# A decoder layer on one core: row dots moved from retrieval into the gate units, a gelu behind one more tile, and fewer row fetches beside two-layer tiles

## The chip, the cores and the metric

The kernel runs on one core of a Trainium2 chip. The core has five engines with instruction streams of their own: TensorE (PE; its weight loads are listed apart as PEld), VectorE (DVE), ScalarE (ACT), GpSimd (POOL) and SyncE (SP, which here only issues transfers). Each works its stream in order and waits for the others by semaphores. The metric is the device time of one execution in microseconds (us).

## The reference, cut to what matters

The layer is a token mixer (pooling, sparse attention, cross-attention) followed by a PEER channel mixer. The change lies in the latter. For 512 tokens and 8 heads it finds the 16 best of 16,384 single-neuron experts, and adds up their outputs:

```python
def block(xb):                       # tokens xb, n of them
    q = (xb @ w_q).reshape(n, PEER_HEADS, 2, PEER_HALF)
    s = jnp.einsum('nhpc,hpkc->nhpk', q, sub_keys)
    s_top, i_top = lax.top_k(s, PEER_TOPK)
    ...                              # the 16 best sums of two halves, their ids
    gate = jax.nn.softmax(best_s, axis=-1)
    u_e = u[ids]
    act = jax.nn.gelu(jnp.einsum('nd,nhkd->nhk', xb, u_e), approximate=False)
    wgt = gate * act
    return jnp.einsum('nhk,nhkd->nd', wgt, v[ids])
x = x + peer_ffn(rms_norm(x, g_ffn), ...)
```

## The kernel before, in words

The kernel computes the PEER mixer in two ways at once. The first 128 tokens (block 0) and, for the first layer only, 48 more tokens are **gathered**: the 128 rows of `u` that a token chose are fetched by indirect transfers, and DVE forms the dot products. For all other tokens (384, less the 48 in the first layer) the mixer is computed **densely**: each of 128 tiles of 128 experts is multiplied with all tokens on PE, and a gate that is zero for every expert not chosen is multiplied in.

A dense tile has a first layer, `hidden` (L172: 24 matmuls of 336 columns, then a gelu on ACT, L1226), and a second layer, 18 matmuls of 512 columns (L1656). Every float32 weight tile is split for PE into a high half `wh` (ACT, L144) and a low half `wl` (DVE or POOL, L145). The first layer of 80 tiles is done ahead, by the generator `lead()`; its results `hg` are stored in `hd`. These are **led tiles**; `step(1)` runs one. They fill PE while DVE does other things. In the last part, `experts()`, the 48 tiles not led come first (**two-layer tiles**), then the 80 led ones, of which only the second layer is left (**one-layer tiles**).

The order of the program around the change is written out by hand:

- *Retrieval.* For each of four blocks of tokens, `retrieve(b)` turns the top-k positions into expert ids on DVE in four pieces (L1342 to L1380); between them `step(1)` runs led tiles. The ids of the 48 tokens go out and come back turned, and POOL gathers their rows `ux` (L1420), 4 buffers ahead.
- *Dots.* `dot_x()` is one DVE instruction of 128x1024 (L1428) that multiplies one such row tile with the tokens and sums it into one column of `actx`; then POOL gathers the row tile four further on. There are 48 dots.
- *Gate units.* The 384 tokens are cut into 12 units of 32. `one_hots` builds one-hot tables on DVE (`oa` L1480, `ob` L1484 and twice L1487), and calls one function after each of the first three. `gates` multiplies them on PE (64 matmuls, L1497) for the unit before, ACT evicts the result (L1500), and a transfer that ACT issues stores it (L1508). Units 0 to 9 are without the 48 tokens (`plain` is 10); unit 9 is the last one before the gelu of `actx` is needed. Units 0 to 6 run five led tiles each, units 7 and 8 four.
- *Gelu of the dots.* `act_x()` is a gelu of `actx` on ACT (L1432). `regroup_x`, `gate_x` and `turn_x` then fold it into the gates of the 48 tokens.
- *Experts.* `weave` runs two generators beside each other, each with a weight: it always continues the one that is least far, by the sum of what it yielded over its weight. `experts()` yields 1.35 twice for a two-layer tile and 1.0 for a one-layer tile. `gathered(0)` yields 1 for each of its 262 row steps: it issues a row gather `ug` on POOL (L1520) and, six steps later, uses the row on DVE, first 128 rows of `u` (dot, L1534), then 128 rows of `v` (added into `x1g`, L1540).

For one tile, `experts()` multiplies the gates with `hg` on DVE (`gh`, L1635), splits the product (`wgh` on ACT L144, `wgl` on DVE L145), and splits the V tile; PE's second layer waits for these. `G` (`gj`, `go`) holds gates that come back from `gd`. The gathers of `gathered` begin behind a POOL copy `seen` that waits for the third V tile.

Of the kernel before, what the change touches and what calls it, by code (L numbers as in the profile page):

```python
# [36 lines left out]
def weave(*streams):  # L37

    live = [[0.0, w, iter(gen)] for gen, w in streams]
    while live:  # L40
        item = min(live, key=lambda x: x[0])
        try:
            c = next(item[2])
            item[0] += (c if c else 1.0) / item[1]
        except StopIteration:
            live.remove(item)
# [7 lines left out]
def seq(*gens):  # L54
    for x in gens:
        yield from x
# [65 lines left out]
def layer(ctx: ExitStack, tc: tile.TileContext, A: dict, out: bass.AP, dbg=None):  # L122
# [88 lines left out]
    GB = 1  # L211
# [3 lines left out]
    LEAD = 80  # L215
# [389 lines left out]
    for c in cross_order:  # L605
        n = int(c[1]) if c[1:].isdigit() else None
# [802 lines left out]
    todo_x, HX, PICK = list(range(X)), {}, []  # L1409
# [13 lines left out]
    def dot_x():  # L1423
        if not todo_x:
            return
        k = todo_x.pop(0)
        row = XR.pop(k)
        v.scalar_tensor_tensor(row, row, 1.0, HX[k >= 32], op0=OP.mult, op1=OP.mult, accum_out=actx[:, k:k + 1])  # L1428
        gather_x(k + XB)

    def act_x():
        s.activation(actx, actx, AF.Gelu)  # L1432
# [37 lines left out]
    def one_hots(u, *others):  # L1470
        others = iter(others)
        tk = slice(u * UT, u * UT + UT)
        full = [128, UT // 2, 128, 2]

        def pairs(x):
            return x.rearrange("p (a w) -> p a w", w=2)[:, :, None].to_broadcast(full)

        every = io128[:, None].to_broadcast(full)
        oa = gp.tile(full, F16, name="oa", bufs=2)
        v.tensor_tensor(oa, pairs(iT[:, tk]), every, op=OP.is_equal)  # L1480
        next(others)()
        ob = gp.tile([128, 2, 4096], F16, name="ob", bufs=2).rearrange(
            "p r (a j w) -> p r a j w", a=UT // 2, j=128)
        v.tensor_tensor(ob[:, 1], pairs(jT[:, tk]), every, op=OP.is_equal)  # L1484
        for r in range(2):
            next(others)()
            v.tensor_tensor(ob[:, r], ob[:, 1], pairs(gT[:, r, tk]), op=OP.mult)  # L1487
        return oa, ob

    def gates(u, oa, ob, then=None):  # L1490
        stg = sgp.tile([128, 64, UT, 2], F32, name="stg", bufs=2)
        for q_ in range(UT // 4):
            pg = psum(("S", "o", "tr")[(u * (UT // 4) + q_) % 3], [128, 4, 128])
            for n in range(4):
                t_ = q_ * 4 + n
                for r in range(2):
                    pe.matmul(pg[:, n], oa[:, t_ // 2, :, t_ % 2], ob[:, r, t_ // 2, :, t_ % 2],  # L1497
                              start=n == 0 and r == 0,
                              stop=n == 3 and r == 1, skip_group_check=True)
            s.activation(stg[:, :, q_ * 4:q_ * 4 + 4].rearrange("p j t c -> p t j c"),  # L1500
                         pg.rearrange("p t (j c) -> p t j c", c=2), AF.Copy, scale=1.0 / 32768.0)
            if then and q_ == 5:
                then()
        if u == 0:
            g.tensor_copy(own, stg[:, LEAD // 2:LEAD // 2 + 4])

        def store():
            s.dma_start((gd[:, :, u - 1] if u else gz).rearrange("j i x -> i j x"),  # L1508
                        stg.rearrange("p (j q) t c -> p j (q t c)", q=4))
        if u == 0:  # L1510
            return store
        store()
# [96 lines left out]
    def experts():  # L1609
        acc_o.extend(psum(("S", "S", "tr", "tr", "o", "o")[i], [128, 512]) for i in range(2 * ND))  # L1610
        for n in range(-1, 128):
            m = n + 1
            if m < 128:
                j = order[m]
                if j >= LEAD:
                    U[m] = feed.take(("u", j))
                vfetch(m + 3)
                hfetch(m + 4)
                if m == 8:
                    bcast_row(gl, A["g_final"])  # L1620
                if m == 100:
                    ex_[0].tile([128, 8], F32, name="pad")
                    for b in range(GB, NB):
                        X1[b] = (X1B if b == GB
                                 else uf.tile([128, D], F32, tag="wr", name="wr", bufs=2))
                        nc.sync.dma_start(X1[b], x1d[b - GB])
                if m % 8 == 4 and m + 4 < 128:
                    gload(m // 8 + 1)
                if j >= LEAD:
                    vpart(m)  # L1630
                    yield 1.35
                    H[m] = hidden(U.pop(m))
                gh = GH.pop() if GH else ex_[0].tile([128, NT], F32, name="gh", bufs=2)
                idle.append(H[m])
                v.tensor_tensor(gh.rearrange("p (g t) -> p g t", t=UT), G[m // 8][:, :, m % 8 // 2, :, m % 2],  # L1635
                                H.pop(m).rearrange("p (g t) -> p g t", t=UT), op=OP.mult)
                if j < LEAD:
                    yield 1.0
                wh = WGH.pop() if WGH else ex_[0].tile([128, NT], F32R, name="wgh", bufs=3)
                wl = ex_[0].tile([128, NT], F32R, name="wgl", bufs=3)  # L1640
                split(wh, wl, gh)
                if j < LEAD:
                    vpart(m)
                V[m] = (wh, wl, V[m])
                if j >= LEAD:
                    yield 1.35
            if n < 0 or n == 126:
                continue

            ends = n == 127  # L1650
            for b in range(ND):
                for k, hs in [(k, (half,)) for half in range(2) for k in (126, 127)] if ends else [(n, range(2))]:
                    wh, wl, vw = V[k]
                    for i, (a, c) in enumerate(((wh, vw[0]), (wl, vw[0]), (wh, vw[1]))):
                        for half in hs:
                            pe.matmul(acc_o[2 * b + half], a[:, b * 128:(b + 1) * 128], c[:, half],  # L1656
                                      start=k == 0 and i == 0, stop=k == 127 and i == 2)
                    if ends and k == 127:
                        closing(GB + b, hs[0])
                        if b and hs[0] == 0:  # L1660
                            finish(GB + b - 1)
                        if b and hs[0]:
                            for half in range(2):
                                output(GB + b - 1, half)
            V.pop(n)
# [12 lines left out]
    def step(n):  # L1678
        for _ in range(n):
            next(ld, None)  # L1680
# [14 lines left out]
    for n, b in enumerate(found):  # L1695
        for i, _ in enumerate(retrieve(b)):
            if n == 0 and i == 1:
                late.append(exp)
            if n or i:
                step(1)  # L1700
            if n == 3 or n == 2 and i:
                dot_x()
            if i in ((2, 3) if n == 0 else (1, 3)):
                piece()
        if n == 0:
            gate_softmax()
            lead_q[0] = nc.sync
        elif found[n - 1] >= GB:
            turn_sel(found[n - 1])
    pend = None  # L1710
# [7 lines left out]
    units = [*range(2, NT // UT), 1, 0]  # L1718
    plain = len(units) - 2
# [4 lines left out]
    def go_dot():  # L1724
        step(1)
        dot_x()

    for n, u in enumerate(units):
        def before():
            if n == plain:  # L1730
                regroup_x()
                gate_x()
            gates(units[n - 1], *pend)
            step(1)
            if n == plain:
                turn_x()

        if n >= plain:
            pend = one_hots(u, go, before, go)
            continue  # L1740
        oh_ = one_hots(u, go, go_dot if n < 7 else dot_x, go)
        if n == 0:
            turn_sel(NB - 1)
            step(1)
        dot_x()
        if n == plain - 1:
            while todo_x:
                dot_x()
        if pend is not None:
            gates(units[n - 1], *pend, act_x if n == plain - 1 else None)  # L1750
        step(1)
        if n < plain - 1:
            dot_x()
            step(1)
            dot_x()
        pend = oh_
    lead_q[0] = s
    step(1)
# [2 lines left out]
    gath = seq(*[gathered(b) for b in range(GB)])  # L1761
# [21 lines left out]
    vfetch(2)  # L1783
    g.tensor_copy(G[0][:, 0], own)
    g.tensor_copy(seen[:, 0:1], VR[2][:, 0:1])
    weave((experts(), 2.7 * (128 - LEAD) + 1.0 * LEAD), (gath, 268 * GB))
    finish(NB - 1)
    for half in range(2):
        output(NB - 1, half)
# [87 lines left out]
```

## Time and profile before

| | us |
|---|---|
| median of 3 runs | 1822.11 (1821.51 to 1822.67) |
| the profiled execution, in all | 1820.59 |
| its span, first to last instruction | 1818.8 |
| PE busy | 1780.1 (98%) |
| DVE busy | 1377.1 (76%) |
| ACT busy | 827.1 (45%) |
| POOL busy | 821.9 (45%) |

The mean granted clock of TensorE is 0.995. By the profile retrieval ends at about 834 us, gate units run to about 1087, the two-layer tiles to about 1478 and the one-layer tiles to the end. All times in the lines below are from the span's start. A line of a timeline has start and duration, engine, line, operation and tile (output<-inputs); in square brackets, the idle time before it and what ended that. A line of waits has who waited for whom, microseconds in total, how many times, and the longest. A line of stretches has the stretch, its length, then for each engine busy microseconds and (the number of instructions), the granted clock, the share of time in which the 16 DMA engines were busy, and GB/s.

### The profile page before, as it was taken

What the parts mean: (1) busy time and instruction counts of PE and PEld (TensorE: products, weight loads), DVE (VectorE), ACT (ScalarE), POOL (GpSimd) and SP (SyncE); (2) the same over time, 40 slices, a digit from 0 to 9 for tenths busy, and PEclk for the clock granted to TensorE, in tenths of its full rate; (3) what the DMA queues carried; (4) which work ended last, traced back from release to release, by engine and by line L of the source; (5) the groups of instructions that cost most, each with busy time, mean ns of one, the idle gap of its engine ahead of it and who ended that gap; (6) DMA issues with size and microseconds to landing.
All of it is one profiled execution on the core that took longest, in us unless ns stands there. A gap on an engine that the chain in (4) does not pass through costs nothing.

```text
span 1818.8 us, 28113 instructions
## 1 busy us (share of the span) xinstructions
PE 1780.1 (98%) x10114; PEld 1566.6 (86%) x10114; DVE 1377.1 (76%) x2846; ACT 827.1 (45%) x1476; POOL 821.9 (45%) x615
## 2 busy tenths in 40 slices
PE   8999999999999999999999899999999999999998
PEld 7988888888888888998999898999888878888886
DVE  5453147766643369999888966999999999999996
ACT  6433257777643433463545453333333333333334
POOL 4333455555643233433333304766766664343320
PEclk9999999999999999999999999999999999999999
DMA  6225622112223432478999989999999999999993
GB/s 224 91 81 178 223 95 65 50 62 59 64 82 116 168 120 94 136 247 277 345 343 340 331 296 379 409 405 378 391 394 387 368 392 406 381 390 388 392 385 105
DMA packets 161950, 456.55 MB, mean 251 GB/s; under 512 B 16513, under 2 KB 64305, under 8 KB 159122
## 3 DMA queue, kind: packets, MB, share of 16 engines
q1 hardware_dynamic: 90354, 264.45, 40.2%
q0 software_dynamic: 44320, 161.03, 23.5%
q10 hardware_dynamic: 27136, 29.26, 4.8%
q8 instruction: 80, 1.31, 0.3%
q14 instruction: 60, 0.49, 0.1%
HBM read 411.82 MB, written 48.10 MB: 253 GB/s over the span
## 4 chain that ended last, share of the span: by engine, by line
PE 66%; DVE 22%; issue 5%; ACT 4%; DMA 2%; POOL 1%; SPq 0%; ACTq 0%; DVEq 0%; POOLq 0%
PE z L172 34%; DVE ug L1534 7%; PE S L1656 6%; PE tr L1656 6%; DVE wl L145 6%; PE o L1656 6%; PE S L916 2%; DVE x1g L1540 2%; PE tr L948 1%; ACT wgh L144 1%; PE o L964 1%; PE S L1177 1%; DVE gh L1635 1%; DMA gd<-stg 1%; PE o L435 1%
## 5 line engine op out<-in xcount | busy, mean ns | idle before, releaser
L144 ACT ACTIVATE wh<-wr 128x1024 fp32r<-128x1024 f32 (+2 forms) x365 | 369.3, 1024 | 136.7 <-PE z L172 38.6
L145 POOL TENSOR_TENSOR wl<-wr,wh 128x1024 fp32r<-128x1024 f32 (+2 forms) x110 | 241.5, 2196 | 319.5 <-ACT wh L144 268.2
L145 DVE TENSOR_TENSOR wl<-wr,wh 128x1024 fp32r<-128x1024 f32 x255 | 306.6, 1218 | 84.6 <-ACT wh L144 83.8
L172 PE MATMUL z<-hfh,wh 128*128 128x336 f32 (+1 forms) x1136 | 363.5, 327 | 5.9 <-ACT wh L144 5.8
L172 PE MATMUL z<-hfl,wh 128*128 128x336 f32 (+1 forms) x1136 | 360.0, 324 | 0.0
L1520 POOL DMA_INDIRECT ug<-in_v_rows_dram,ids x128 | 174.4, 1362 | 194.2 <-DVE x1g L1540 178.3
L144 ACT ACTIVATE wgh<-gh 128x384 fp32r<-128x384 f32 x128 | 67.3, 526 | 396.6 <-DVE gh L1635 389.8
L1520 POOL DMA_INDIRECT ug<-in_u_rows_dram,ids x128 | 198.5, 1551 | 85.0 <-DVE ug L1534 64.5
L172 PEld LDWEIGHTS z<-hfh,wh 128*128 128x128 f32 x1136 | 214.2, 189 | 14.0 <-ACT wh L144 7.4
L172 PEld LDWEIGHTS z<-hfl,wh 128*128 128x128 f32 x1136 | 214.3, 189 | 6.5
L172 PE MATMUL z<-hfh,wl 128*128 128x336 f32 (+1 forms) x1136 | 207.6, 324 | 5.6 <-DVE wl L145 5.6
L172 PEld LDWEIGHTS z<-hfh,wl 128*128 128x128 f32 x1136 | 182.0, 188 | 13.8 <-DVE wl L145 8.3
L1420 POOL DMA_INDIRECT ux<-in_u_rows_dram,idx x48 | 99.8, 2079 | 148.7 <-DVE ux L1428 143.4
L1540 DVE SCALAR_TENSOR_TENSOR x1g<-ug,wgt,x1g 128x1024 f32<-128x1024 f32 x128 | 164.0, 1281 | 1.2
L1534 DVE SCALAR_TENSOR_TENSOR ug<-ug,hf 128x1024 f32<-128x1024 f32 x128 | 152.3, 1219 | 7.0 <-DMA ug<-in_u_rows_dram,ids 6.9
L172 PE MATMUL z<-hnh,wh 128*128 128x512 f32 x384 | 150.8, 393 | 0.0
L172 PE MATMUL z<-hnl,wh 128*128 128x512 f32 x384 | 150.3, 391 | 0.0
L1226 ACT ACTIVATE hg<-z 128x336 f32<-128x336 f32 x128 | 56.8, 444 | 157.7 <-PE z L172 157.4
L937 POOL TENSOR_SCALAR pr<-pr,sm,gsig 128x128 f32<-128x128 f32 (+3 forms) x128 | 78.0, 613 | 77.9 <-DVE sm L1011 47.4
L952 DVE TENSOR_TENSOR PB<-tr,PB 128x128 fp32r<-128x128 f32 (+3 forms) x128 | 62.6, 489 | 49.1 <-ACT PB L951 48.6
L172 PE MATMUL z<-hnh,wl 128*128 128x512 f32 x384 | 99.3, 393 | 0.0
L145 DVE TENSOR_TENSOR wgl<-gh,wgh 128x384 fp32r<-128x384 f32 x128 | 71.5, 559 | 32.4 <-ACT wgh L144 32.4
(417 smaller groups left out, 3623.2 us busy)
## 6 DMA issues: line engine op xcount, KB each, us to landing
wr<-in_u_t_dram SPq DMA_DIRECT2D x128, 512.0 KB, 6.5
wr<-in_v_rows_dram SPq DMA_DIRECT2D x128, 512.0 KB, 9.2
wr<-in_w_z_dram SPq DMA_DIRECT2D x48, 512.0 KB, 3.6
gd<-stg ACTq DMA_DIRECT2D x11, 2048.0 KB, 13.2
hg<-hd SPq DMA_DIRECT2D x80, 168.0 KB, 9.5
hd<-hg SPq DMA_DIRECT2D x68, 168.0 KB, 6.6
gj<-gd SPq DMA_DIRECT2D x8, 1408.0 KB, 10.8
go<-gd SPq DMA_DIRECT2D x8, 1408.0 KB, 12.1
```

What stands on the lines that cost most here:

```text
L144: s.activation(hi, src, AF.Copy)
L145: (eng or v).tensor_tensor(lo, src, f(hi), op=OP.subtract)
L172: pe.matmul(p, w[a][:, k], xs(x[b], k), start=k == 0 and a == 0 and b == 0, stop=k == nk - 1 and a == 1)
L916: pe.matmul(sp[:, 0:nn], Q[gq, r][:, qb * 128:(qb + 1) * 128], KK[gq, br][i][:, 0:nn], start=i == 0, stop=i == 1)
L937: g.tensor_scalar(pr[:, 0:n], pr[:, 0:n], sm, gsig[:, qb, c:c + 1], op0=OP.mult, op1=OP.mult)
L952: return lambda: v.tensor_tensor(lo, pt[:, 0:qb + 1], f(hi), op=OP.subtract)
L1226: s.activation(hg[:, X:], p[:, X:NT], AF.Gelu)
L1420: g.indirect_dma_start(out=XR[k], out_offset=None, in_=A["u_rows"], in_offset=bass.IndirectOffsetOnAxis(ap=idx[:, k:k + 1], axis=0))
L1520: g.indirect_dma_start(out=row, out_offset=None, in_=src, in_offset=bass.IndirectOffsetOnAxis(ap=ids[:, b, k:k + 1], axis=0))
L1534: v.scalar_tensor_tensor(row, row, 1.0, hf[:, b], op0=OP.mult, op1=OP.mult, accum_out=act[:, m:m + 1])
L1540: v.scalar_tensor_tensor(X1[b], rows.pop(m), wgt[:, m - 128:m - 127], X1[b], op0=OP.mult, op1=OP.add)
L1656: pe.matmul(acc_o[2 * b + half], a[:, b * 128:(b + 1) * 128], c[:, half], start=k == 0 and i == 0, stop=k == 127 and i == 2)
```

## The change

Three things change. Two dots instead of seven are placed in retrieval. Units 1 to 8 get five dots each instead of four: one more right after `oa`. Unit 9 no longer empties the list of dots in a row, and the gelu of the dots is not issued among the unit's evictions but behind the led tile that follows them; one more led tile then follows the gelu. Third, `experts()` yields 1.15 twice for a two-layer tile instead of 1.35, and its weight follows (2.3 instead of 2.7 for each of the 48).

```diff
@@ experts()
                 if j >= LEAD:
                     vpart(m)
-                    yield 1.35
+                    yield 1.15
                     H[m] = hidden(U.pop(m))
...
                 if j >= LEAD:
-                    yield 1.35
+                    yield 1.15
@@ retrieval
-            if n == 3 or n == 2 and i:
+            if n == 3 and i % 2:
                 dot_x()
@@ gate units
+    def dot_go():
+        dot_x()
+        step(1)
+
...
-        oh_ = one_hots(u, go, go_dot if n < 7 else dot_x, go)
+        oh_ = one_hots(u, dot_go if n else go, go_dot if n < 7 else dot_x, go)
         if n == 0:
             turn_sel(NB - 1)
             step(1)
         dot_x()
-        if n == plain - 1:
-            while todo_x:
-                dot_x()
         if pend is not None:
-            gates(units[n - 1], *pend, act_x if n == plain - 1 else None)
+            gates(units[n - 1], *pend)
         step(1)
         if n < plain - 1:
             dot_x()
             step(1)
             dot_x()
+        else:
+            assert not todo_x
+            act_x()
+            step(1)
@@ the weave of the last part
-    weave((experts(), 2.7 * (128 - LEAD) + 1.0 * LEAD), (gath, 268 * GB))
+    weave((experts(), 2.3 * (128 - LEAD) + 1.0 * LEAD), (gath, 268 * GB))
```

What this does to the streams shows at three places. First DVE in retrieval, in the third block's ids (`e` are its one-hot tables, `wl` the low halves of led tiles):

```order
 L1360 TENSOR_TENSOR e<-ab,io 128x2048 x2
 L145 TENSOR_TENSOR wl<-wr,wh 128x1024
-L1428 SCALAR_TENSOR_TENSOR ux,actx<-ux,hfx 128x1024
 L1364 TENSOR_TENSOR e<-e,sif 128x4096
 L145 TENSOR_TENSOR wl<-wr,wh 128x1024
-L1428 SCALAR_TENSOR_TENSOR ux,actx<-ux,hfx 128x1024
 L1368 TENSOR_TENSOR e<-e 128x16x128
 L1368 TENSOR_TENSOR e<-e 128x16x64
```

Here two dots leave the stream between the low halves; three more leave further on.

Then DVE in gate unit 9, from its `oa` to the low halves behind it; before:

```order
L1480 TENSOR_TENSOR oa<-iT,io_6437 128x4096
L145 TENSOR_TENSOR wl<-wr,wh 128x1024
L1484 TENSOR_TENSOR ob<-jT,io_6437 128x4096
L1428 SCALAR_TENSOR_TENSOR ux,actx<-ux,sv 128x1024
L1487 TENSOR_TENSOR ob<-ob,gT 128x4096
L145 TENSOR_TENSOR wl<-wr,wh 128x1024
L1487 TENSOR_TENSOR ob<-ob,gT 128x4096
L1428 SCALAR_TENSOR_TENSOR ux,actx<-ux,sv 128x1024 x4
L145 TENSOR_TENSOR wl<-wr,wh 128x1024
```

and now, the same stretch:

```order
L1480 TENSOR_TENSOR oa<-iT,io_6437 128x4096
L1428 SCALAR_TENSOR_TENSOR ux,actx<-ux,sv 128x1024
L145 TENSOR_TENSOR wl<-wr,wh 128x1024
L1484 TENSOR_TENSOR ob<-jT,io_6437 128x4096
L1428 SCALAR_TENSOR_TENSOR ux,actx<-ux,sv 128x1024
L1487 TENSOR_TENSOR ob<-ob,gT 128x4096
L145 TENSOR_TENSOR wl<-wr,wh 128x1024
L1487 TENSOR_TENSOR ob<-ob,gT 128x4096
L145 TENSOR_TENSOR wl<-wr,wh 128x1024 x2
```

The last dot now stands ahead of the first multiplication by `gT`; before, four stood behind the second one. On ACT the gelu of the dots stands in that unit; before, among the evictions:

```order
 L1500 ACTIVATE stg<-o 128x4x64x2
+L1500 ACTIVATE stg<-tr 128x4x64x2
+L1500 ACTIVATE stg<-S 128x4x64x2
+L1508 DMA gd<-stg 128x16x256
+L144 ACTIVATE wh<-wr 128x1024
+L1226 ACTIVATE hg_6446<-z 128x336
 L1432 ACTIVATE actx<-actx 128x48
-L1500 ACTIVATE stg<-tr 128x4x64x2
-L1500 ACTIVATE stg<-S 128x4x64x2
```

It moves behind the unit's last two evictions, their store, and one led tile's `wh` and gelu.

Last DVE in the two-layer tiles, at the third of them (`gh` begins a tile's product; `wl` x2 are the low halves of a V and a U tile; L1534 are the rows):

```order
 L1635 TENSOR_TENSOR gh<-gj,hg_6447 128x384
 L145 TENSOR_TENSOR wgl<-gh,wgh 128x384
-L1534 SCALAR_TENSOR_TENSOR ug,act<-ug,hf 128x1024 x2
+L1534 SCALAR_TENSOR_TENSOR ug,act<-ug,hf 128x1024
 L145 TENSOR_TENSOR wl<-wr,wh 128x1024 x2
 L1534 SCALAR_TENSOR_TENSOR ug,act<-ug,hf 128x1024 x2
```

Here a tile has three rows where it had four. Beside the two-layer tiles stand 148 rows in all instead of 158, and 20 of `v` instead of 30; the other ten stand beside one-layer tiles.

## The prediction

> **What bounds the kernel now.** I read the page's head first, then a table of stretches that I cut by stage, then who waits for whom in the stretches where TensorE (PE) falls short. From the page:
>
> ```profile
> span 1818.8 us, 28113 instructions
> PE 1780.1 (98%) x10114; PEld 1566.6 (86%) x10114; DVE 1377.1 (76%) x2846; ACT 827.1 (45%) x1476; POOL 821.9 (45%) x615
> ```
>
> PE is busy for 98% of the span, but a matmul that crawls at a lowered clock also counts as busy. So I look for stretches with few weight loads per microsecond (PEld, the count in brackets). The rows are retrieval, two gate units, the first two-layer tiles, the last ones and the one-layer tiles:
>
> ```profile
> core 0: us, PE busy (x) PEld busy (x) DVE busy (x) ACT busy (x) POOL busy (x), PEclk, DMA share, GB/s
> 804.98:851.65 46.67, 41.06 (x257) 38.62 (x256) 46.26 (x61) 17.32 (x23) 17.36 (x12) 1.00 0.81 255
> 866.50:888.66 22.16, 22.16 (x186) 22.02 (x185) 19.76 (x18) 11.45 (x18) 8.89 (x5) 1.00 0.94 330
> 995.64:1014.10 18.46, 18.46 (x162) 18.34 (x161) 18.12 (x17) 9.95 (x16) 9.38 (x5) 1.00 1.02 372
> 1136.89:1272.90 136.01, 136.01 (x740) 123.56 (x739) 125.37 (x190) 48.29 (x70) 93.76 (x61) 1.00 1.01 398
> 1407.50:1478.70 71.20, 67.26 (x352) 58.51 (x351) 65.38 (x66) 23.87 (x36) 49.71 (x31) 1.00 1.00 382
> 1500.00:1740.00 240.00, 240.00 (x1060) 198.73 (x1059) 217.88 (x253) 93.52 (x118) 95.46 (x77) 1.00 1.01 393
> ```
>
> In retrieval VectorE (DVE) works 46.26 of 46.67 us while PE loses 5.6: DVE sets the pace there. In the gate units PE is full and DVE has room, 2.4 us in the long unit and 0.3 in the short one. In the last two-layer tiles DVE rules again; in the one-layer tiles PE is full and DVE idles 22 of 240 us. So the change is worth what PE waits for DVE, directly or through ScalarE (ACT), in the places it touches. I take them in order of time.
>
> **Retrieval: five dots leave (gain 5.3).** The waits between 800 and 855 us, and DVE's timeline there:
>
> ```profile
> PEld z L172 <- DVE wl L145: 8.0, 9, 2.0
> ```
> ```profile
> 817.58 1.22 DVE L145 TENSOR_TENSOR wl<-wr,wh 128x1024 fp32r<-128x1024 f32 x1
> 818.72 1.22 DVE L1428 SCALAR_TENSOR_TENSOR ux<-ux,hfx 128x1024 f32<-128x1024 f32 x1
> ...
> 819.86 2.36 DVE L1360 TENSOR_TENSOR e<-ab,io 128x2048 f16<-128x2048 f16 x2
> 822.13 1.22 DVE L145 TENSOR_TENSOR wl<-wr,wh 128x1024 fp32r<-128x1024 f32 x1
> ```
>
> PE waits 8.0 us, nine times, for the low half (wl) of a led tile, always behind DVE. A dot (L1428) holds DVE from 818.72 to 819.86, 1.14 us. Five dots leave: 5 x 1.14 = 5.7. DVE hardly idles, so all of it should reach PE; less than that only if a wl then waits for ACT instead. Bounds 3 and 5.7; I take 5.3, near the top. About 2.5 us of waiting stay, late next is the wl behind the first one-hot. The gathers of rows follow their dots, POOL only issues them.
>
> **Gate units: one dot more in each (cost 0.4).** Units 1 to 8 get one more dot. In the long unit DVE has 22.16 - 19.76 = 2.4 us of room for 1.14: hidden behind PE. In the short one 18.12 + 1.14 = 19.26 against 18.46, so DVE runs 0.8 over; there are two such units, and the one before them refills DVE's lead. Bounds 0 and 1.6, I take 0.4. If that cover fails, wl is late and each unit pays.
>
> **The gelu of the dots (gain 7.5).** Before, the last unit empties the list of dots and the gelu (L1432) stands among ACT's evictions. The waits between 1033 and 1056 us, and led tiles (L172) in two stretches of the same kernel:
>
> ```profile
> ACT actx L1432 <- DVE ux L1428: 6.5, 1, 6.5
> PEld z L172 <- ACT wh L144: 5.8, 1, 5.8
> ```
> ```profile
> 1046.20:1051.60 5.40, 5.40 (x24) 5.19 (x24) 0.68 1.02 321
> 1068.31:1083.09 14.78, 11.29 (x74) 11.03 (x72) 1.00 0.79 261
> ```
>
> ACT stands 6.5 us for four dots in a row; queued behind it are two evictions, the store and the high half (wh) of the next led tile, so PE is idle for 5.8 us. Then the granted clock is 0.68 and 24 weight loads take 5.40 us, where 72 take 11.03 elsewhere (3.68 for 24): another 1.7. In the changed order only two dots are in that unit, both ahead of DVE's last one-hot multiplication, and the gelu follows a whole led tile. It waits for nothing. Gain 5.8 + 1.7 = 7.5; the lower bound is 4, if a row comes late.
>
> [...] The rows below show 0.69 and 0.79 after gaps of 2.9 and 2.2 us, so here I go by the rows.
>
> **Start of the two-layer tiles (gain 3.0).** The waits between 1100 and 1137 us, and the expert matmuls (L1656) of two tiles:
>
> ```profile
> POOL seen L1785 <- DMA wr<-in_v_rows_dram: 17.6, 1, 17.6
> ...
> DVE ug L1534 <- DMA ug<-in_u_rows_dram,ids: 6.9, 4, 3.1
> ...
> PEld S L1656 <- ACT wgh L144: 2.9, 1, 2.9
> ```
> ```profile
> 1131.31:1136.89 5.58, 5.58 (x18) 4.36 (x18) 0.69 1.03 411
> 1140.63:1144.67 4.04, 3.88 (x18) 3.35 (x18) 1.00 1.05 428
> ```
>
> DVE stands 6.9 us for the first row fetches, PE then 2.9, and the clock takes 5.58 - 4.04 = 1.5 more. Now one row less stands ahead of the tile that waits. But the led tile that moved ahead of the gelu no longer covers this start: expert work comes 3.7 us sooner after the last gates. Its U load and its store of hg move along on SP's queue, now ahead of the loads of the first V tiles, about 0.7 MB less behind the gates. The third V tile and with it the row fetches come sooner too, the store of the last gate unit does not. Bounds: all is gained (4.4), or the tile's whole 3.7 becomes waiting. I take 3.0, since the fetches wait for that V tile and move with the tiles.
>
> **Two-layer tiles (gain 8.3).** The weights 2.7 to 2.3 make the row steps per two-layer tile 2.7 x 268 / 209.6 = 3.45 before and 2.3 x 268 / 190.4 = 3.24 now; per one-layer tile 1.28 and 1.41. Waits from 1137 to 1474 us, then from 1474 to 1500; DVE's timeline from one gh to the next, first in the u rows, then in the v rows; and weight loads of L1656 just after the change to one layer and later:
>
> ```profile
> PEld S L1656 <- ACT wgh L144: 3.2, 4, 0.8
> PEld S L1656 <- DVE wgl L145: 3.1, 11, 0.3
> ```
> ```profile
> PEld S L1656 <- ACT wgh L144: 2.2, 1, 2.2
> ```
> ```profile
> 1389.66 0.56 DVE L1635 TENSOR_TENSOR gh<-gj,hg 128x384 f32<-128x384 f32 x1
> ...
> 1396.99 0.56 DVE L1635 TENSOR_TENSOR gh<-gj,hg 128x384 f32<-128x384 f32 x1
> ```
> ```profile
> 1430.38 0.55 DVE L1635 TENSOR_TENSOR gh<-go,hg 128x384 f32<-128x384 f32 x1
> ...
> 1435.46 2.60 DVE L1540 SCALAR_TENSOR_TENSOR x1g<-ug,wgt,x1g 128x1024 f32<-128x1024 f32 x2
> 1437.98 0.55 DVE L1635 TENSOR_TENSOR gh<-go,hg 128x384 f32<-128x384 f32 x1
> ```
> ```profile
> 1478.70:1486.80 8.10, 8.10 (x28) 6.33 (x29) 0.79 0.96 349
> 1600.00:1608.10 8.10, 8.10 (x37) 6.74 (x36) 1.00 1.03 406
> ```
>
> Both timelines hold three rows: 7.33 us with u rows, 7.60 with v rows (a pair of these takes 1437.98 - 1435.46 = 2.5). A u row has the dot's form, 1.14; a v row costs about 1.3. PE needs 136.01 us for 739 loads, 42 a tile (24 + 18): 7.73 us. At 3.45 rows DVE needs 7.33 + 0.45 x 1.14 = 7.84, over PE; in v rows 7.60 + 0.45 x 1.3 = 8.19. At 3.24 it is 7.60 and 7.91: under PE for u rows, 0.2 over for v rows. The switch to v rows also comes later: 20 of them stand beside two-layer tiles instead of 30, with one tile of four rows. DVE saves up a lead before that and spends little of it. What can be won is 3.2 + 3.1 in the waits, 2.2 at the change to one layer (where PE suddenly wants the next tile four microseconds sooner), and the clock after it: seven loads fewer in 8.10 us, 7 x 8.10 / 36 = 1.6. In all 10.1; below, if DVE saves no lead, only the 6.3 less a third, 4. I take 8.3, since DVE's sum falls below PE's for most of the stretch.
>
> **One-layer tiles (0).** PE needs 240 x 18 / 1059 = 4.08 a tile; DVE works 217.88 of 240 us, 3.70 a tile. 0.13 rows more are 0.13 x 1.3 = 0.17: 3.87, hidden behind PE. Without that cover it would be 80 x 0.17 = 13.6 us.
>
> **Sum.** 5.3 - 0.4 + 7.5 + 3.0 + 8.3 = 23.7 us. The profiled execution took 1820.6 us in all (1.8 beside its span), 1.5 under the median of 1822.1. From the median: 1798.4.
>
> **Rivals.** *The start is uncovered:* the moved led tile turns into 3.7 us of waiting and nothing of the 4.4 goes: 23.7 - 3.0 - 3.7 = 17.0, 1805. For it: the first rows already came late. Against: they move with the tiles.
>
> *The gate units are full of transfers.* Fetches there run at a share of 0.94 to 1.02. If that were a ceiling, one row of 0.52 MB more at about 350 GB/s would lengthen each of eight units by 1.5 us: 12.0 of the gain is lost, 1810. Against: other stretches move 393 to 411 GB/s, and PE hardly stands for a transfer there.
>
> *Slower: the transfer rate of today is a ceiling everywhere.* Then the gate units lose 12.0, the start gains nothing (3.0), and the ten row fetches that go to one-layer tiles cost 10 x 0.52 / 0.393 = 13.3 there: 23.7 - 28.3 = -4.6, 1827. It decides once the ceiling is under 400 GB/s: the short unit needs 372 + 28, the one-layer tiles 393 + 17. Against: 411 and 428 stand in the rows above.
>
> [...]
>
> *It does not do what it says:* waits only change places, within 0.2%.
>
> **How the numbers follow.** Chances: forecast 0.62, uncovered start 0.20, full gate units 0.10, no change 0.05, ceiling everywhere 0.03. Predicted is the first, 1798.4. The best case, all upper bounds, is 5.7 + 7.5 + 4.4 + 10.1 = 27.7, or 1794. The range 1794 to 1810 reaches to the second rival. 0.2% (3.6 us) is about what a measurement can tell from no change: faster 0.92, same 0.05, slower 0.03.
>
> **What would show it.** Retrieval: PE's wait for wl falls from 8.0 to about 2.5. Gelu: no wait of ACT for the dots, no clock under 0.9 near 1040. Start: the wait for wgh before the fourth expert tile gone or under 1.5, or, if I am wrong, longer. Two-layer tiles: PE's waits for wgh and wgl under 2 in all, and no gap at the change to one layer. One-layer tiles: 4.08 a tile as before; if they take 4.2, the third rival holds. I am wrong if gate units exceed 22.2 or 18.5 us by a microsecond.

## The result, and the profile after

The changed kernel takes 1795.49 us (median of 4 runs, 1794.88 to 1799.73), the kernel before 1822.39 in the same series: a ratio of 0.9857 (95% interval 0.9840 to 0.9874), 26.9 us less. The forecast was 1798.4. The profiled execution took 1794.88 us in all; its page begins:

```profile
span 1793.1 us, 28115 instructions
PE 1770.9 (99%) x10114; PEld 1564.5 (87%) x10114; DVE 1375.9 (77%) x2846; ACT 833.8 (47%) x1476; POOL 823.9 (46%) x615
```

PE still counts 10114 matmuls, in 25.7 us less. (The profiled execution of the kernel before lies 1.8 us under its median, that of the changed kernel 0.6 us, so the traces have 25.7 us to divide and not 26.9.) The stretches that answer to the prediction's are, in this order: retrieval, a long and a short gate unit, unit 9's evictions and the gelu, the fourth expert tile, two-layer tiles (early, late), the first 8.1 us of one-layer tiles, and one-layer tiles later on:

```profile
core 0: us, PE busy (x) PEld busy (x) DVE busy (x) ACT busy (x) POOL busy (x), PEclk, DMA share, GB/s
804.98:851.65 46.67, 45.52 (x296) 44.73 (x295) 46.26 (x58) 20.08 (x27) 13.12 (x10) 1.00 0.76 232
860.70:882.84 22.14, 22.14 (x186) 22.02 (x185) 20.71 (x20) 11.59 (x18) 10.36 (x6) 1.00 0.98 359
989.83:1008.28 18.45, 18.45 (x162) 18.33 (x161) 18.45 (x18) 10.05 (x16) 10.54 (x5) 1.00 1.04 381
1030.38:1046.66 16.28, 16.28 (x163) 16.00 (x161) 13.01 (x13) 9.00 (x17) 0.00 (x0) 1.00 0.85 299
1119.30:1123.38 4.08, 4.08 (x28) 3.96 (x26) 3.49 (x7) 1.62 (x3) 2.69 (x2) 1.00 1.03 413
1130.00:1266.00 136.00, 136.00 (x735) 123.18 (x734) 125.94 (x188) 50.63 (x71) 92.02 (x58) 1.00 1.01 399
1383.00:1454.18 71.18, 71.18 (x385) 64.39 (x384) 64.83 (x75) 25.05 (x36) 44.71 (x29) 1.00 0.99 381
1454.18:1462.28 8.10, 8.10 (x37) 6.74 (x36) 8.03 (x11) 2.96 (x4) 6.06 (x4) 1.00 0.91 324
1600.00:1700.00 100.00, 100.00 (x443) 82.80 (x442) 93.52 (x108) 39.28 (x50) 44.73 (x35) 1.00 1.03 404
```

Read the granted clock and the loads together: it is 1.00 in every row, and the last two-layer tiles now make 384 loads in 71.18 us where 351 stood in 71.20. Retrieval makes 295 where 256 stood. The long gate unit keeps its 22.14 us with DVE at 20.71; in the short one DVE is full (18.45 of 18.45) and PE still needs only 18.45. In the one-layer tiles the transfers moved from 393 to 404 GB/s.

To divide the 25.7 us I put markers on the trace: the first weight load of `gates` in units 1 and 9 (64 loads a unit) and of expert tiles, counted by their 18 loads each (S0 is the first two-layer tile, S47 the last one, S120 a late one-layer tile). Times from the span's start:

| marker | before | changed | gained in this stretch |
|---|---|---|---|
| gates in unit 1 | 866.5 | 860.7 | 5.8 |
| gates in unit 9 | 1033.1 | 1026.8 | 0.5 |
| S0 | 1105.1 | 1091.5 | 7.3 |
| S4 | 1140.6 | 1123.4 | 3.6 |
| S46 | 1472.5 | 1450.1 | 5.1 |
| S47 | 1478.7 | 1454.2 | 2.2 |
| S51 | 1496.9 | 1470.6 | 1.7 |
| S120 | 1778.4 | 1752.2 | 0.0 |
| end | 1818.8 | 1793.1 | -0.5 |

Waits of the changed kernel, first in retrieval (795 to 846 us), then in unit 9 (1020 to 1050), and ACT's timeline at the gelu of the dots:

```profile
PEld z L172 <- DVE wl L145: 1.9, 3, 1.1
```
```profile
ACT wh L144 <- DMA wr<-in_u_t_dram: 2.8, 1, 2.8
```
```profile
1034.42 0.45 ACT L1226 ACTIVATE hg<-z 128x336 f32<-128x336 f32 x1 [0.81 <-PE z L172]
1034.77 0.23 ACT L1432 ACTIVATE actx<-actx 128x48 f32<-128x48 f32 x1
```

The gelu (L1432) has no bracket: it waits for nothing and takes 0.23 us. ACT's wait for dots is gone from the list; what ACT waits for now is a U load, and PE does not stop for it. At the start of the two-layer tiles (1080 to 1125 us):

```profile
POOL seen L1790 <- DMA wr<-in_v_rows_dram: 13.8, 1, 13.8
...
DVE ug L1534 <- DMA ug<-in_u_rows_dram,ids: 5.6, 1, 5.6
...
PEld S L1656 <- ACT wgh L144: 0.6, 1, 0.6
```

The first row fetches still come late (5.6 us for DVE), but only 0.6 of it reaches PE. In the 330 us of two-layer tiles after that PE waits for neither `wgh` nor `wgl`; the 42 tiles from S4 to S46 take 326.76 us, 7.78 each, which is what PE alone needs.

### The profile page after: what moved, and what is told of

Read it like the earlier page. It is cut to its first block, busy times and chain, and to the rows that moved or that the text cites. A ratio compares the mean times of both kernels' runs of the same rounds, so it can differ in the third digit from the quotient of the medians.

```text
span 1793.1 us, 28115 instructions
## 1 busy us (share of the span) xinstructions
PE 1770.9 (99%) x10114; PEld 1564.5 (87%) x10114; DVE 1375.9 (77%) x2846; ACT 833.8 (47%) x1476; POOL 823.9 (46%) x615
## 4 chain that ended last, share of the span: by engine, by line
PE 89%; DVE 4%; ACT 3%; DMA 1%; issue 1%; POOL 0%; SPq 0%; DVEq 0%; ACTq 0%; POOLq 0%
PE z L172 47%; PE S L1656 9%; PE tr L1656 9%; PE o L1656 9%; PE S L916 2%; PE tr L948 1%; PE o L964 1%; PE S L1177 1%; PE o L435 1%; ACT pr L929 1%; PE o L1497 1%; PE tr L1497 1%; PE S L1497 1%; PE o L1261 1%; ACT wh L144 1%
## 5 line engine op out<-in xcount | busy, mean ns | idle before, releaser
L1534 DVE SCALAR_TENSOR_TENSOR ug<-ug,hf 128x1024 f32<-128x1024 f32 x128 | 152.3, 1217 | 5.6 <-DMA ug<-in_u_rows_dram,ids 5.6
```

The costliest lines, as they stand in the source:

```text
L1534: v.scalar_tensor_tensor(row, row, 1.0, hf[:, b], op0=OP.mult, op1=OP.mult, accum_out=act[:, m:m + 1])
```

## The experiments

Each kernel was timed in three rounds beside the kernel before, whose median was 1823.0 to 1823.8 us in these series. Differences "to the changed kernel" are of medians, against 1795.49.

**1. The parts.** Only the weights, on the kernel before:

```diff
-                    yield 1.35        (twice)
+                    yield 1.15
-    weave((experts(), 2.7 * (128 - LEAD) + 1.0 * LEAD), (gath, 268 * GB))
+    weave((experts(), 2.3 * (128 - LEAD) + 1.0 * LEAD), (gath, 268 * GB))
```

> The kernel before with the new weave weights alone (1.15 and 2.3). Theory: DVE's sum per two-layer tile falls under PE's 7.78 us, so PE's waits there (6.3 us), the gap at the change to one layer (2.2) and the lowered clock after it (1.6) go, and a part of the wait at the start: 8.5 to 10.5 us less, about 1813. Rival: these waits went because the rows and tiles came earlier once the dots had moved; then the weights alone give 4 us or less, 1818 or more, and PE's wait at the change to one layer stays above 1 us.

Measured: 1813.08 us, ratio 0.9940 (0.9923 to 0.9956), 10.0 less than before. From S46 to S47 it takes 4.04 us, as in the changed kernel; S0 to S4 takes 32.3 (before 35.6, changed 31.9). So the weights alone bring nearly all of the gain in the two-layer tiles (S4 to S46 takes 327.3 us, before 331.8, changed 326.8), at the change to one layer and at the start. The gate units of this kernel are those of before, and the profiled execution shows their stop (1015 to 1060 us):

```profile
PEld z L172 <- ACT wh L144: 9.3, 2, 5.9
...
ACT actx L1432 <- DVE ux L1428: 6.6, 1, 6.6
...
ACT wh L144 <- DMA gd<-stg: 4.7, 1, 4.7
```

The 5.9 are the dots' gelu again; the other 3.4 of the 9.3 are a wait of ACT for the store of a gate unit, which the traces of the kernel before and of the changed one do not have.

Only dots and gelu, that is the changed kernel with the weights of before:

```diff
-                    yield 1.15        (twice)
+                    yield 1.35
-    weave((experts(), 2.3 * (128 - LEAD) + 1.0 * LEAD), (gath, 268 * GB))
+    weave((experts(), 2.7 * (128 - LEAD) + 1.0 * LEAD), (gath, 268 * GB))
```

> The changed kernel with the old weave weights (1.35 and 2.7): only the dots, the gelu and the led tile are moved. Theory: 5.7 in retrieval, 0.5 in the gate units, 7.3 at the gelu and 1 to 3 at the start: 14.5 to 16.5 us less, about 1807; the waits in the two-layer tiles stay as before (6 us, then 2.2). Rival, the uncovered start: the led tile that moved is missed before the experts and PE's wait there grows by up to 3.7 us, so only 10 us less, 1812.

Measured: 1806.42 us, ratio 0.9913 (0.9896 to 0.9930), 16.6 less than before. The two parts add up: 10.0 + 16.6 = 26.6, where both together bring 26.9. The waits of the two-layer tiles stay (1125 to 1490 us):

```profile
PEld S L1656 <- ACT wgh L144: 6.5, 9, 2.2
PEld S L1656 <- DVE wgl L145: 5.0, 17, 0.4
```

From S46 to S47 it takes 6.23 us as before. The start, however, is short here too: 32.2 from S0 to S4, with four rows still ahead of the tile that waits. So either edit shortens it, and together they do it once, not twice.

**2. The gelu of the dots.** Two edits could remove the stall: dots that are done early, or a gelu that is not ahead of `wh`. First, the gelu back among the evictions, the dots as changed; then the gelu moved, the dots as before (four in a row in unit 9):

```diff
-            gates(units[n - 1], *pend)
+            gates(units[n - 1], *pend, act_x if n == plain - 1 else None)
...
-            act_x()
             step(1)
```

> The changed kernel with the gelu of the dots back among the evictions of the last gate unit, the dots and the extra led tile as changed. Theory A: what stopped ACT was four dots in a row behind the last one-hot product; now the last dot ends before the evictions begin, so the gelu waits for nothing wherever it stands: 1795.5 within 1. Theory B: it is the place of the gelu in ACT's stream that counts: PE stands 5.8 us again and loses clock, 1802 to 1803.

Measured: 1795.88 us, ratio 0.9854 (0.9835 to 0.9872): the same as the changed kernel. The gelu stands among the evictions again, and it does not wait, since its last dot is long done.

```diff
-            gates(units[n - 1], *pend, act_x if n == plain - 1 else None)
+            gates(units[n - 1], *pend)
         step(1)
+        if n == plain - 1:
+            act_x()
```

> The kernel before with only the gelu moved behind the led tile that follows the last unit's gates; the four dots still stand in a row on DVE. Theory B (place of the gelu): ACT evicts, stores and splits on; PE's 5.8 us and the 1.7 of clock shrink to the 1 to 2 us that a late low half costs behind the row of dots: 5 to 7 us less, 1816. Theory A (the row of dots itself): DVE is held 4.6 us, low halves come as late as before, 0 to 2 us less, 1820 or more.

Measured: 1815.51 us, ratio 0.9961 (0.9947 to 0.9975), 7.5 less than before. Its waits in 1015 to 1060 us:

```profile
ACT actx L1432 <- DVE ux L1428: 2.4, 1, 2.4
PEld z L172 <- DVE wl L145: 1.9, 1, 1.9
```

ACT waits 2.4 instead of 6.5, behind a led tile, and PE no longer for `wh`; 1.9 us go to a `wl` behind the four dots. So the stall needs both, late dots and a gelu in front of `wh`. The two edits are not of equal worth, though. From the gates in unit 9 to S0 the kernel before takes 72.0 us and the changed one 64.7; the early dots alone reach 64.7 as well, the later place alone 66.5, which is 5.5 of the 7.3 us. (The 7.5 us by the medians are not this stretch alone.) In the changed kernel the later place is insurance.

**3. The led tile that moved.** The changed kernel without the extra led tile behind the gelu (it runs where it ran before):

```diff
             act_x()
-            step(1)
```

> The changed kernel without the extra led tile behind the gelu; the tile stands again before the experts. Theory (nothing waits for the gelu, and the first rows of the experts move along with the tiles): the same time within 1 us. Rival, the uncovered start: the tile covers the start of the experts, whose wait (0.8 us now) goes; the same or 0.8 less. If instead the wait at the start returns to 3 us or more, the moved tile was itself what shortened it: 2.5 to 3.5 us more.

Measured: 1796.02 us, ratio 0.9861 (0.9839 to 0.9882): the same. S0 to S4 takes 32.6 us against 31.9. PE's wait at the start is 1.2 us instead of 0.6, and the total does not tell the two apart: in the changed kernel the tile neither covers the start nor uncovers it by more than that.

**4. Two dots in retrieval, or none.** No dots in retrieval; the two go to unit 9, the last of them right ahead of the gelu, with one low half between them:

```diff
-            if n == 3 and i % 2:
-                dot_x()
...
-            assert not todo_x
+            while todo_x:
+                dot_x()
```

> The changed kernel with no dot in retrieval; the two go to the last unit, one of them behind the led tile and right ahead of the gelu. Theory: PE's remaining waits for low halves near 830 to 845 us (1.9 us) shrink to 0.5 or less, since DVE comes 2.3 us sooner to the first one-hots; the gelu waits some 1 us on ACT and PE does not: 1.5 us less than the changed kernel. Rival: what is left there is the first one-hots' own cost, nothing changes, or the late dots stop ACT again, 3 us more or worse.

Measured: 1795.76 us, ratio 0.9844 (0.9828 to 0.9861): the same. The gates of unit 1 begin at 859.2 instead of 860.7 us, but the last of their loads start at 1076.8 and 1076.7: the 1.5 us are given back, where late dots make the gelu wait again (1005 to 1060 us). The expectation had the gelu wait 1 us and PE not at all; it was 2.8 and 1.2:

```profile
ACT actx L1432 <- DVE ux L1428: 2.8, 1, 2.8
...
PEld z L172 <- ACT wh L144: 1.2, 2, 0.7
```

**5. How far the weights go.** Rows moved on, from two-layer to one-layer tiles, where the changed kernel has 1.41 a tile. Weights 1.0 and 2.0 give 1.52 rows, weights 0.8 and 1.6 give 1.71:

```diff
-                    yield 1.15        (twice)
+                    yield 1.0         (0.8)
-    weave((experts(), 2.3 * (128 - LEAD) + 1.0 * LEAD), (gath, 268 * GB))
+    weave((experts(), 2.0 * (128 - LEAD) + 1.0 * LEAD), (gath, 268 * GB))      (1.6)
```

> The changed kernel with 1.0 and 2.0 as weights: 3.05 row steps per two-layer tile, 1.52 per one-layer tile (3.24 and 1.41 in the changed kernel). Theory: the two-layer tiles already run at PE's pace, and a one-layer tile costs DVE 3.30 us with one row and 4.60 with two, 3.98 on the mean, still under PE's 4.08: the time of the changed kernel within 1.5 us. Rival, the transfer rate is a ceiling: 1.52 rows per 4.08 us ask for some 420 GB/s, so one-layer tiles take 4.2 us or more and the run 8 us more.

> The changed kernel with 0.8 and 1.6 as weights: 2.74 row steps per two-layer tile, 1.71 per one-layer tile. Theory: DVE needs 0.29 x 3.30 + 0.71 x 4.60 = 4.22 us per one-layer tile, over PE's 4.08, so PE waits there for wgh and wl: 8 to 11 us more than the changed kernel, about 1805, with DVE busy nearly all the time. Rival (PE alone sets the end, rows are hidden in one-layer tiles): no change. Rival (transfers): the same or more time, but DVE idle, waiting for ug or hg by transfer.

Measured: 1804.85 us (ratio 0.9897, 0.9880 to 0.9911) and 1820.66 us (0.9987, 0.9977 to 0.9996), 9.4 and 25.2 more than the changed kernel. My theory, that a one-layer tile has room on DVE and so room for the rows, failed on the first by 8 us, and the 8 to 11 us expected of the second became 25.2. Waits of the first from 1500 to 1790 us and its stretch 1600 to 1700:

```profile
DVE gh L1635 <- DMA wr<-in_v_rows_dram: 8.6, 1, 8.6
PEld S L1656 <- ACT wh L144: 7.8, 3, 7.4
```
```profile
1600.00:1700.00 100.00, 92.76 (x395) 75.31 (x394) 87.74 (x102) 33.03 (x44) 46.69 (x34) 0.95 1.03 407
```

Transfers run at 407 GB/s and DVE is not full. From 1500 to 1600 us PE still works 99.93 us, up to 1687 us it never waits more than 0.7 us, and then it stands for 7.4 us at once, with a granted clock of 0.95 over these 100 us. DVE's timeline shows where it stops, and the transfers issued from 1670 to 1695 us show what came late (size, and us from issue to landing):

```profile
1692.06 0.56 DVE L1635 TENSOR_TENSOR gh<-go,hg 128x384 f32<-128x384 f32 x1 [8.62 <-DMA wr<-in_v_rows_dram]
```
```profile
go<-gd SPq DMA_DIRECT2D x1, 1408.0 KB, 18.3
...
go<-gz SPq DMA_DIRECT2D x1, 128.0 KB, 17.4
```

The list of waits names a V tile, but `gh` reads no V tile. It reads `go`, the gates of eight tiles, and this is the first of the eight. Their load is issued four tiles ahead, which is 16.3 us at 4.08 a tile, here behind three loads of 0.5 MB (`x1d`); it landed at 1691.9 us, and `gh` started at 1692.1. In the changed kernel the same load took 16.8 us and landed some 0.1 us before `gh` came. With weights 0.8 both long stops, of 3.9 and 7.8 us, also stand at the first tile of such a group, the longer one again behind the three loads. So the long stop is a late gate load; whether the rate of the transfers made it late is tried below. The time from issue to landing of V tiles in 1500 to 1700 us tells that the ceiling is near before PE waits (minimum, median, maximum; before, changed, weights 1.0, weights 0.8):

```profile
DMA to landing us min/median/max: 5.1/9.2/16.1
```
```profile
DMA to landing us min/median/max: 6.9/11.9/17.7
```
```profile
DMA to landing us min/median/max: 7.4/13.9/17.6
```
```profile
DMA to landing us min/median/max: 9.1/15.9/19.0
```

To separate DVE from transfers, both kernels once more with every second row fetch left out; DVE reads the row before it again, so its stream is the same:

```diff
-                rows[n] = gather(todo[n][0], b, todo[n][1])
+                rows[n] = rows[n - 1] if n % 2 else gather(todo[n][0], b, todo[n][1])
```

> The weights 1.0 and 2.0 with half of the row fetches: every second gather is left out and DVE uses the row before it again, so DVE does the same work and about 67 MB of row fetches (half of 256 rows of 0.52 MB) are not moved; what the rows are worth to the result is lost with them. Theory T (the 9.4 us that the weights 1.0 and 2.0 lost against the changed kernel were transfers): the stop of 7.8 us and the clock after it go, 1794 to 1797 us, and the share of the DMA engines in the one-layer tiles falls to about 0.8 to 0.85. Theory V (VectorE): no change, 1803 to 1806, since VectorE's stream is the same.

> The weights 0.8 and 1.6 (1.71 rows beside a one-layer tile) with half of the row fetches; every second row is used twice, so VectorE's work is unchanged. It divides the 25 us that these weights lost against the changed kernel. Theory T: with transfers halved only VectorE is left over the tile: 0.30 rows more than in the changed kernel at about 1.3 us each on 3.8 us of work a tile give 4.2 against 4.08, so 1800 to 1806 us with PE waits for wl and wh spread over many tiles and none over 2 us. Theory V: VectorE is all of it, 1818 to 1822.

Measured: 1793.84 us (0.9837, 0.9820 to 0.9853) and 1806.02 us (0.9904, 0.9887 to 0.9920). The stretch 1600 to 1700 us of the one and of the other, and the second one's wait of PE in 1450 to 1790 us:

```profile
1600.00:1700.00 100.00, 100.00 (x443) 82.81 (x442) 97.62 (x112) 39.43 (x50) 24.15 (x18) 1.00 0.92 333
```
```profile
1600.00:1700.00 100.00, 99.37 (x429) 79.45 (x428) 99.43 (x113) 34.38 (x48) 27.04 (x20) 1.00 0.93 334
```
```profile
PEld S L1656 <- DVE wl L145: 15.5, 35, 0.6
```

With weights 1.0 DVE works 97.62 of 100 us and PE loses nothing: all 9.4 us were transfers. (With fewer gathers POOL was also less busy, 24.15 us instead of 46.69 of the 100, but 46.69 is far from full. The share of the DMA engines fell to 0.92, less far than the 0.80 to 0.85 expected.) The gate load that had come late, of 17.4 us to landing for its last part, now takes 14.6. With weights 0.8 DVE is full at 99.4, a tile takes 100 x 18 / 429 = 4.20 us instead of 4.08, and 80 tiles lose 10 us: the 10.5 measured. The other 14.6 of the 25.2 went with the fetches. With all its rows both limits show in that kernel, in the waits from 1457 to 1790 us (two long ones and a short one for `wh`, the long ones where gates came late; 25 small ones for `wl` of DVE) and in the stretch 1600 to 1700:

```profile
PEld S L1656 <- ACT wh L144: 12.3, 3, 7.8
PEld S L1656 <- DVE wl L145: 12.1, 25, 0.6
```
```profile
1600.00:1700.00 100.00, 96.26 (x409) 78.19 (x408) 95.73 (x108) 34.75 (x46) 58.59 (x40) 0.97 1.03 407
```

An estimate from the rows: 0.30 rows of 0.524 MB in 4.08 us are 38.5 GB/s on top of 404, so 442 are asked where 407 are moved; over the 326 us of 80 tiles that is 28 us. For weights 1.0 the same sum (0.11 rows, 418 asked) gives 9. By this estimate transfers alone could account for the 25.2, and DVE's 10 is not added to them but runs beside them; how the 25.2 divide is not shown.

**6. Room in the gate units.** The changed kernel with a transfer of 0.5 MB, of no use, beside each of units 1 to 8:

```diff
+        if 0 < n < 9:
+            nc.sync.dma_start(junk[n], A["v_rows"][n * 128:(n + 1) * 128])
         dot_x()
         if pend is not None:
```

> The changed kernel and beside each of the gate units 1 to 8 one transfer of 0.5 MB more, from memory to memory, of no use. It asks how much room the gate units have for transfers, the prediction's second rival. If units at 360 to 380 GB/s have the room up to about 407 that the one-layer tiles reach: 0.5 MB in 18 to 22 us is 24 to 28 GB/s more, which just fits, 1794 to 1798 us, the gate units' transfer rate rises. If they are full: each unit gets about 1.3 us longer, 1804 to 1808.

Measured: 1807.34 us, ratio 0.9907 (0.9891 to 0.9924), 11.9 more than the changed kernel. My expectation that 407 GB/s holds here as well failed. The stretch 866 to 1030 us of the kernel before, the changed one and this one:

```profile
866.00:1030.00 164.00, 163.71 (x1385) 162.50 (x1384) 145.30 (x131) 85.42 (x137) 66.20 (x32) 1.00 0.98 346
```
```profile
866.00:1030.00 164.00, 164.00 (x1383) 162.99 (x1383) 153.87 (x145) 85.41 (x135) 72.50 (x36) 1.00 1.01 372
```
```profile
866.00:1030.00 164.00, 157.87 (x1275) 155.87 (x1274) 143.74 (x136) 80.25 (x128) 69.30 (x36) 0.97 1.00 367
```

and the waits of the last from 840 to 1060 us:

```profile
ACT wh L144 <- DMA wr<-in_u_t_dram: 38.1, 12, 5.3
...
PEld z L172 <- ACT wh L144: 8.1, 6, 3.4
```

The rate does not rise, 367 against 372; U tiles come late instead, and PE stops six times. 8 x 0.524 MB at 372 GB/s are 11.3 us. The loss is not spread over the units, as I had expected, but stands mostly in two of them: unit 3 takes 27.0 us where it took 22.1, unit 6 takes 24.6 where it took 18.5. So the room between 346 and 372 was there for one row a unit, and there was none for this transfer. Whether a second row would find none is open in two points: this transfer goes from memory to memory and not into the core, and it is issued on SP's queue among the U loads, which a row fetch is not.

One dot more in units 1 and 2, none in retrieval:

```diff
-            if n == 3 and i % 2:
-                dot_x()
...
-        oh_ = one_hots(u, dot_go if n else go, go_dot if n < 7 else dot_x, go)
+        oh_ = one_hots(u, dot_go if n else go, go_dot if n < 7 else dot_x, go_dot if 0 < n < 3 else go)
```

> The changed kernel with no dots in retrieval; gate units 1 and 2, which run five led tiles, take one dot more each. VectorE's 2.3 us leave retrieval, of which an earlier run showed about 1.5 reaching PE; the units have 1.2 us of VectorE's room left each for 1.14. If that holds: 1.0 to 1.5 us less than the changed kernel, 1793.5 to 1795, less than a measurement can tell from no change; the marker where gate units begin comes 1.5 us sooner and this stays until the end. If the room is used up: the gain is given back in units 1 and 2.

Measured: 1797.59 us, ratio 0.9855 (0.9838 to 0.9871): no gain. Unit 1 begins 1.0 us sooner, units 1 to 4 keep their 22.1 to 22.2 us, and unit 5 takes 26.0. The waits there (940 to 985 us):

```profile
ACT wh L144 <- DMA wr<-in_u_t_dram: 7.9, 5, 4.2
...
PEld z L172 <- ACT wh L144: 2.4, 1, 2.4
```

DVE's room was there, and what stopped PE was a late U tile, as in the run before. That the two rows of units 1 and 2 cause the stop of unit 5 is consistent with it (860 to 948 us runs at 372 GB/s instead of 366), but is not shown. The 2.1 us more are less than the executions of the changed kernel differ among themselves, and a kernel with the very gate units of the changed one, that of weights 0.8 and 1.6, has such a stop in its profile too. Its unit 4 takes 27.0 us instead of 22.1 (waits from 926 to 955 us):

```profile
ACT wh L144 <- DMA wr<-in_u_t_dram: 9.0, 3, 5.2
...
PEld z L172 <- ACT wh L144: 3.4, 1, 3.4
```

So a U tile can come too late in the changed gate units without any transfer more. In the profile of the changed kernel itself ACT waits for U tiles eight times, 8.0 us in all (840 to 1060 us; before, twice and 2.0 us), and PE does not stop. No version that was run and does the whole work beats the changed kernel.

## Why the prediction was right, step by step

| term | forecast | measured |
|---|---|---|
| retrieval | 5.3 | 5.8 |
| gate units | -0.4 | +0.5 |
| gelu of the dots | 7.5 | 7.3 |
| start of the two-layer tiles | 3.0 | 3.6 |
| two-layer tiles, the change to one layer, the clock after it | 8.3 | 5.1 + 2.2 + 1.7 = 9.0 |
| one-layer tiles | 0 | 0.0, end -0.5 |
| sum | 23.7 | 25.7 |

**Retrieval.** Five dots of 1.14 us reach PE in full, a little over the upper bound; 1.9 us of waiting for `wl` stay where 2.5 were forecast.

**Gate units.** The sign was wrong. The cost of 0.4 came from the short unit, where DVE was to run 0.8 over. DVE is indeed full there (18.45 of 18.45 us) and does 18 instructions where it did 17, while a dot is recorded as two, so part of the added work ran beyond the stretch; PE lost nothing, since the lead of DVE, for which the lower bound allowed, covered all of it. The gain of 0.5 is a wait of 0.6 us in unit 8 that the kernel before had. What the sum of this step left out, and only the second rival named, was the resource that was really short: after the change transfers in the units stand at 372 GB/s and a share of 1.01, U tiles come later, and 0.5 MB more a unit cost 11.9 us in experiment 6.

**Gelu of the dots.** Size and place were right: 7.3, with neither ACT's wait nor a lowered clock left (1.00 from 1030 to 1080 us, before 0.93). But only half of the reason was told: the prediction named dots and place in one breath, and experiment 2 shows that the early dots alone are enough, while the place alone brings 5.5.

**Start.** 3.6, between the 3.0 taken and the 4.4 bound. PE's wait is 0.6 of the 1.5 allowed. The reason given, one row fewer ahead of the waiting tile, is sufficient (weights alone: 32.3 us) but not necessary (dots alone: 32.2 us). Why the second shortens it is settled in part. In the kernel before DVE waits for the first rows four times, 6.9 us in all; with the dots and the tile moved it waits 5.7 us, 5.2 of them at once. With the moved tile back (experiment 3) DVE waits four times again (6.6 us in all, 3.8 the longest) and S0 to S4 takes 0.7 us more. This points at the tile, but that run has the changed weights, which shorten the start by themselves; what the tile is worth with four rows ahead was not tried.

**Two-layer tiles.** The mechanism held: with fewer rows a tile all of PE's waits for DVE's products went (6.3 us from 1137 to 1474 before, none from 1120 to 1455 now; PE needs 7.78 us a tile, not the 7.73 worked out), and with the gap at the change to one layer the clock's loss went too: 36 loads in the first 8.1 us instead of 29. The 8.3 were 0.7 too few, because less was left of the waits than allowed for.

**Clock.** Before, gaps of 2.9 and 2.2 us were each followed by a clock of 0.69 and 0.79, and with the gaps these are gone; 1.7 us came back at S47 to S51 alone. That is not so after every short gap: in the kernel with only the gelu moved, a gap of 2.1 us at S3 was followed by 1.00. Before, in retrieval, PE's weight loads stopped for 1.97 us up to 838.57 us, and the clock from 838 to 840 us read 1.00 as well. Going by the rows was right for the two gaps that they show; which gaps lower the clock, the runs do not tell.

**Rivals.** The uncovered start did not come: where the tile stands changes the total by nothing that shows (experiment 3). The full gate units: the mechanism exists, and with one transfer of a row's size more it costs 11.9 us, close to what the rival asked for (12.0), though in two units and not in eight; the rows of before, 346 GB/s over all units, did not tell where it begins. The ceiling everywhere: it exists too, at 407 GB/s in the one-layer tiles, and was to decide under 400. The changed kernel asks for 404 to 406, and moved 406 from 1500 to 1600 us and 404 from 1600 to 1700. It escaped this rival by less than 1%, and that was luck: no row of before told 407 from 430. With weights 1.0 the ceiling takes 9.4 us, and the rows of 411 and 428 GB/s over 4 to 6 us, which the prediction set against it, say nothing of what can be sustained: over 100 us the one-layer tiles moved 407 at most.

## What to carry to other kernels

Before moving work to where an engine has room, ask also for room in transfers there, and judge it by how the time from issue to landing grows (here the median for V tiles went from 9.2 to 11.9 us before PE waited) and by the rate over 100 us or more, not by peaks of a few microseconds (411 and 428 GB/s here, where the one-layer tiles moved 407 at most over 100 us). In this kernel a stage stood within 1% of its ceiling, 404 to 406 of 407, without one wait of PE in the list, and 0.11 rows a tile more then cost 9.4 us, where the estimate from the rows is 9. Where such a stage stops, look for the transfer with the tightest deadline, which the list of waits need not name: here it named a V tile, and late was a gate load of 1.5 MB. The stall at the gelu of the dots needed two things, a late input and something urgent queued behind it on ACT. Taking away the late input was enough (64.7 us from the gates in unit 9 to S0, as with both), taking away the queue brought 5.5 of 7.3 us, and one experiment for each told which. When two generators are woven by weights, look for the weight at which the engine that paces the dear tiles just falls under the bound, and stop there: here with 1.15 PE no longer waited for DVE's products from 1120 to 1455 us, and 1.0 cost 9.4 us.

## What the runs showed of the hardware

- Transfers of a mix of row fetches and tiles ended at 407 GB/s in the one-layer tiles, whatever was asked (1.52 or 1.71 rows a tile); the early two-layer tiles of the changed kernel moved 410 from 1100 to 1200 us. In the gate units, over the 164 us from 866 to 1030, they moved 346 before, 372 in the changed kernel, 375 without dots in retrieval (experiment 4) and 367 with 0.5 MB more a unit (experiment 6). In the gate units packets are smaller: 32082 packets for 60.98 MB in 164 us of the changed kernel, 1.9 KB each, against 26013 for 80.99 MB, 3.1 KB each, in 200 us of one-layer tiles. That the size is the reason was not tried.
- With weights 1.0, where by estimate 418 GB/s were asked and 407 moved, the ceiling did not show as many small stops: PE worked 99.93 of the 100 us from 1500 to 1600, never waited more than 0.7 us up to 1687 us, and then stood 7.4 us at once, at the first tile that needed a gate load of 1.5 MB, 17.4 us after its last part was issued.
- The share of busy DMA engines hardly told how near the ceiling was: it read 1.01 at 393 GB/s before, and 1.03 at 404 without a wait of PE and at 407 with stops.
